# Sixteen DRAM-to-DRAM weight-sum transfers, each tied to one dense unit of the mLSTM stage through an unused column

## The chip, the cores and the metric

The kernel runs on one core of a Trainium2 chip. The metric is device time in microseconds (us), the median of several executions. A core has five engines that run side by side, each through its own instructions in order: TensorE (PE in the profile, its weight loads PEld), VectorE (DVE), ScalarE (ACT), GpSimd (POOL) and SyncE (SP), which here only issues transfers. GpSimd issues transfers too. All transfers share the core's 16 DMA engines; those of SyncE lie in queue q1, those of GpSimd in queue q0.

## The reference

One layer of a streaming encoder for 1024 prompt tokens and 64 sample tokens, 1088 columns in all, with 1024 channels, in float32. Cut to what matters:

```
u    = rmsnorm(x, norm1_g) * (1 + sc1) + sh1          # adaLN: sh, sc, g from silu(c) @ w_ada
proj = u @ w_in                                        # q k v | mq mk | mv mo | i f | ga gb
y_a  = stick_breaking(q, k, v)                         # 8 heads of 64
conv = silu(b_conv + causal width-4 conv of (mq mk))
h    = mlstm(conv_q, conv_k, mv, i, f)                 # 4 heads of 128, running max, chunks
y_b  = sigmoid(mo) * rmsnorm(h) * ml_norm_g
x    = x + g1 * ((sigmoid(ga) * (y_a @ w_a) + sigmoid(gb) * (y_b @ w_b)) @ w_out)
u2   = rmsnorm(x, norm2_g) * (1 + sc2) + sh2
x    = x + g2 * ((silu(u2 @ w_ff_gate) * (u2 @ w_ff_up)) @ w_ff_down)
y    = rmsnorm(x, final_g)
```

The products of the FFN's gate and up matrices (1024 x 2816 each) are computed with seven half-size products in place of eight. Four of the seven need weights that are sums of halves: S1 = up's upper half + up's lower half, S2 = S1 + gate's upper half, S3 = up's upper half + gate's upper half, S4 = S2 + gate's lower half.

## The kernel before, in words

Each matmul is three float32r matmuls (mm3, L76 to L78): high part by high part, high by low, low by high. A *dense unit* (`unit`, L340) computes 128 output channels for all 1088 columns. It loads its weights (`w_unit`, SyncE, tile wr), splits them on GpSimd into wh and wl (L53, L59), and runs 3 chunks of 320, 384 and 384 columns, 24 matmuls each, into one of three PSUM banks of tag d. An `evac` function empties each bank. wr, wh and wl have three buffers each, so the split of a unit waits until TensorE has finished the unit three places earlier, and the load of a unit waits for the split of the unit three places earlier.

The mLSTM stage is the loop over four heads h at L908. The generator `mlstm(h)` does the recurrence of head h (W is its decay table, hn its output, hsq the squares for its norm, ps_yb the transposes of its result) while the dense units q, k, v of attention pair h and mq, mk, mv, mo of head h+1 run as filler (`chain(dense)`; in the last head two adaLN blocks and two gate units take the place of the latter). In TensorE's order the units are thus q0 k0 v0 mq1 mk1 mv1 mo1 q1 k1 v1 mq2 and so on. mq and mk are emptied into xp by ScalarE, and VectorE copies their last three columns before the padding into cvo (L687 from the first chunk, L688 at the end). k, v, mv and mo are emptied by ScalarE into kf, vf, mvf and mog.

For a change of heads, W (one buffer) is loaded from nm_d at L725, as a broadcast of 1152 rows of 512 bytes, as soon as the last read of the W before it is done. VectorE's dc (L727, L728) reads it, then GpSimd adds a mask (L730, nine pieces), ScalarE takes dc (L731) and nine exponentials (L733). Between these, in ScalarE's order, stand the three copies of mo's banks into mog (L713).

The FFN's weight sums for the first ten blocks of 128 channels are made by the DMA engines alone, from DRAM to DRAM: `sum_copy` (L158) copies a half matrix of 512 x 1280 into wsum_d[x], `sum_add` (L168) adds another to it (a transfer with accumulation), each in two transfers of 512 x 640, 1280 KB. Sixteen in all, from GpSimd's queue. So that they don't all start at the beginning, each copy is preceded by a transfer of one element of cvo into the place that the copy overwrites, from the same queue: the copy must wait for it, and it must wait for cvo. The adds have no such element; they wait for the copies. They are placed in the code behind units of heads 1 to 3. The FFN reads wsum_d in `load_pair` (L1250), 80 loads of 256 KB.

The order on each engine isn't that of the code: a scheduler sorts all instructions by priority and its own estimates, and adds the waits.

Of the kernel before, what the change touches and what calls it, by code (L numbers as in the profile page):

```python
# [8 lines left out]
F32 = mybir.dt.float32  # L9
F32R = mybir.dt.float32r  # L10
AF = mybir.ActivationFunctionType
ALU = mybir.AluOpType
AX = mybir.AxisListType

P = 128
NS = 64
NP = 1024
T = NS + NP
D = 1024
# [16 lines left out]
def trunk(ctx, tc, a, o, dbg=None, stop=None):  # L36
    nc = tc.nc
# [5 lines left out]
    dram = ctx.enter_context(tc.tile_pool(name="scr", bufs=1, space=bass.MemoryType.DRAM))  # L43
# [27 lines left out]
    def cols(w, c0, n=P):  # L71

        return w[:, c0 : c0 + n].rearrange("(kb p) n -> p kb n", p=P)
# [20 lines left out]
    w_g, w_u, w_d = a["w_ff_gate"][0], a["w_ff_up"][0], a["w_ff_down"][0]  # L94
# [25 lines left out]
    cvo = const.tile([P, 48], F32, name="cvo")  # L120
# [30 lines left out]

    KH = D // 2
    NFC = NF * P
    wsum_d = {x: dram.tile([KH, NFC], F32, name=f"wsum{x}_d") for x in (1, 2, 3, 4)}
    g1w, g2w, u1w, u2w = w_g[0:KH, 0:NFC], w_g[KH:D, 0:NFC], w_u[0:KH, 0:NFC], w_u[KH:D, 0:NFC]
    sum_parts = {1: (u1w, u2w), 2: (g1w, wsum_d[1]), 3: (u1w, g1w), 4: (g2w, wsum_d[2])}

    def sum_copy(x, b):  # L158

        def go():  # L160
            for c in range(0, NFC, NFC // 2):
                nc.gpsimd.dma_start(wsum_d[x][0:1, c : c + 1], cvo[0:1, b : b + 1])
                nc.gpsimd.dma_start(wsum_d[x][:, c : c + NFC // 2], sum_parts[x][0][:, c : c + NFC // 2])
            return
            yield
        return go()

    def sum_add(x):  # L168
        def go():
            for c in range(0, NFC, NFC // 2):  # L170
                nc.gpsimd.dma_start(wsum_d[x][:, c : c + NFC // 2], sum_parts[x][1][:, c : c + NFC // 2], accum_op=ALU.add)
            return
            yield
        return go()

    def small(shape, name, tag, dtype=F32, bufs=2, pool=None):
        return (pool or cur["sb"]).tile(shape, dtype, tag=tag, name=name, bufs=bufs)
# [135 lines left out]
    pairs = [Pair() for _ in range(4)]  # L313
    heads = [Pair() for _ in range(4)]
# [504 lines left out]
    def qkv_units(p):  # L819
        return [in_unit(f"q{p}", OFF_Q + P * p, (p, 0), evac_qk, alloc_qk),  # L820
                in_unit(f"k{p}", OFF_K + P * p, (p, 1), evac_qk, alloc_qk), k_post(p),
                in_unit(f"v{p}", OFF_V + P * p, (p,), evac_v, alloc_v), v_post(p)]

    def ml_units(h):
        return [in_unit(f"mq{h}", OFF_MQ + P * h, (h, 0), evac_x, alloc_x),
                in_unit(f"mk{h}", OFF_MK + P * h, (h, 1), evac_x, alloc_x),
                in_unit(f"mv{h}", OFF_MV + P * h, (h,), evac_mv, alloc_mv),
                in_unit(f"mo{h}", OFF_MO + P * h, (h,), evac_mo, alloc_mo)]
# [8 lines left out]
    def chain(gens):  # L837
        for g in gens:
            yield from g

    def run(consumer, dense, nsteps, nd):

        n = 0.0
        done = False
        if nd == 0:
            for _ in consumer:
                pass
            done = True
        for _ in dense:
            n += nsteps / max(nd, 1)  # L850
            while n >= 1.0 and not done:
                n -= 1.0
                done = next(consumer, "end") == "end"
        for _ in consumer:
            pass
# [49 lines left out]
    for u in [gates_if()] + ml_units(0)[2:]:  # L905
        for _ in u:
            pass
    for h in range(4):  # L908
        q_, k_, kp, v_, vp = qkv_units(h)
        m_ = ml_units(h + 1) if h < 3 else ada_left[0:2] + gates[0:2]  # L910
        b_ = [[], [sum_copy(1, 1), sum_copy(3, 5), sum_add(1), sum_add(3)], [sum_copy(2, 2), sum_copy(4, 6), sum_add(2)],
              [sum_add(4)]][h]
        dense = []
        for i, g in enumerate([q_, k_, kp, v_, vp] + m_):
            dense += [g] + (b_[i // 2 : i // 2 + 1] if i % 2 == 0 else [])
        run(mlstm(h), chain(dense), 14, 23 if h < 3 else 17)
    ps = bank("t", "ps_cvo", 3)
    nc.tensor.transpose(ps[:48, 0:P], cvo, ident)
# [97 lines left out]
    for m in range(KB):  # L1016
        if m % 2 == 0:
            wh, wl = wide_unit(w_a, 0, 4, m // 2, f"wa{m}")
        for c, (s, e) in enumerate(CHUNKS):
            n = e - s  # L1020
# [10 lines left out]
            for lo, hi in ([(s, HT), (HT, e)] if s < HT < e else [(s, e)]):  # L1031
                h = lo // HT
                src, r = gts[0][:, lo - s : hi - s], slice(lo - HT * h, hi - HT * h)
# [216 lines left out]
    def load_pair(i):  # L1250

        def half(w, r):
            return w[r * KH : (r + 1) * KH, i * P : (i + 1) * P].rearrange("(k p) n -> p k n", p=P)

        res = {}
        if i >= NF:
            raws = []
            for w, nm in ((w_g, "g"), (w_u, "u")):
                raw = wp.tile([P, KB, P], F32, tag="wr", name=f"wr_{nm}{i}")
                nc.sync.dma_start(raw, cols(w, i * P))  # L1260
                raws.append(raw)
            res[1], res[2], res[0], res[4] = raws[0][:, 0:4], raws[0][:, 4:8], raws[1][:, 0:4], raws[1][:, 4:8]
            return res
        src = {1: half(w_g, 0), 6: half(wsum_d[2], 0), 5: half(wsum_d[1], 0), 7: half(wsum_d[3], 0),
               2: half(w_g, 1), 3: half(wsum_d[4], 0), 4: half(w_u, 1)}
        for k in range(4):
            if k < 3:
                raw = wp.tile([P, KB, P], F32, tag="wr", name=f"wr_{k}_{i}")
            else:
                raw = gp.tile([P, 4, P], F32, tag="S1", name=f"wr_{k}_{i}", bufs=1)  # L1270
            for x, p in enumerate(order[2 * k : 2 * k + 2]):
                res[p] = raw[:, 4 * x : 4 * x + 4]
                nc.sync.dma_start(res[p], src[p])
        return res
# [88 lines left out]
    slices = [list(range(NF + 4 * i, NF + 4 * i + 4)) for i in range(3)] + [[0, 1, 2, 3], [4, 5, 6, 7], [8, 9]]  # L1363
    jobs = [(i, (0,)) for i in range(NF)] + [(i, (0, 1)) for i in range(NF, FFB)] + [(i, (1,)) for i in range(NF)]
    raw = load_pair(0)
    ws = {p: weight_op(0, p, raw) for p in order}

# [4 lines left out]
    for k, (i, halves) in enumerate(jobs):  # L1372
        nxt, nxt_i = {}, jobs[k + 1][0] if k + 1 < len(jobs) else None
        if k == FFB:
            todo = chain([early_h(b) for b in slices[0]])

        def hook(p, last):
            if last and raw:
                nxt[p] = weight_op(nxt_i, p, raw)
            if (k < NF and p in (6, 2)) or (k >= FFB and p == 5):  # L1380
                step(todo)

        for h in halves:
            if h == halves[-1]:
                raw = load_pair(nxt_i) if nxt_i is not None else None
            gate_up(i, h, ws, lambda p: hook(p, h == halves[-1]))
        ws = nxt
        if k == NF - 1:
            for _ in todo:
                pass  # L1390
# [74 lines left out]
    sums = {}  # L1465
# [102 lines left out]
```

## Time and profile before

| | us |
|---|---|
| median of 3 runs (1866.32 to 1869.25) | 1866.44 |
| the profiled execution | 1861.14 |
| its span, first to last instruction | 1859.4 |

| in the span | |
|---|---|
| mean granted TensorE clock | 0.979 |
| moved by the DMA engines | 265.51 MB, 143 GB/s |
| share of the 16 DMA engines, queue q1 (SyncE) | 41.1% |
| share of the 16 DMA engines, queue q0 (GpSimd) | 9.0% |

The difference between the execution's time and its span, 1.7 us, lies outside the instructions. The slices of the page (40 of 46.5 us each) show in tenths how busy TensorE and the DMA engines are and the granted clock:

```
PE   6899799999989999988998999999999999999997
PEclk9999899999999999998999999999999999999999
DMA  9427749423485565684566345622222666443102
```

Counted from 0, the mLSTM stage is slices 2 to 10. Of these, TensorE is below 9 tenths in slice 4, and there the clock is lower as well. Idle time of another engine costs nothing while TensorE has work.

### The profile page before, as it was taken

The numbers are of one execution on the slowest core, as the hardware profiler recorded it, in microseconds if no ns is written. First come the engines' busy times: TensorE is split into PE (matmuls) and PEld (weight loads), VectorE is DVE, ScalarE is ACT, GpSimd is POOL, SyncE is SP. The second block draws the span as 40 slices with busy tenths as digits, with TensorE's granted clock in tenths as the row PEclk, the third lists the DMA queues.
The fourth block names the chain that finished last, engine by engine and source line by source line (L and its number), as shares of the span: only waits on it lengthen the run. The fifth ranks groups of instructions, "written<-read, shape, count | busy, mean of one in ns | idle before, by whom it ended". The sixth has DMA issues, their size and how long they took to land. (4 is left out here: it accounts for less than half of the span.)

```text
span 1859.4 us, 31695 instructions
## 1 busy us (share of the span) xinstructions
PE 1763.3 (95%) x12388; PEld 1695.7 (91%) x12388; DVE 995.4 (54%) x1903; ACT 673.5 (36%) x1403; POOL 678.2 (36%) x562
## 2 busy tenths in 40 slices
PE   6899799999989999988998999999999999999997
PEld 4799799899979888877898999999999999999997
DVE  6623314133355758696554389665445776544535
ACT  4433322434234435353412456433233553100006
POOL 3434445335432232368566240032222002354324
PEclk9999899999999999998999999999999999999999
DMA  9427749423485565684566345622222666443102
GB/s 273 104 88 193 193 118 259 131 83 118 128 173 142 136 141 152 157 231 157 156 201 195 93 144 169 197 88 82 86 71 76 194 203 189 168 146 110 55 12 97
DMA packets 313433, 265.51 MB, mean 143 GB/s; under 512 B 13895, under 2 KB 285507, under 8 KB 313283
## 3 DMA queue, kind: packets, MB, share of 16 engines
q1 hardware_dynamic: 300994, 224.67, 41.1%
q0 software_dynamic: 12288, 38.80, 9.0%
q8 instruction: 98, 1.61, 0.4%
q14 instruction: 53, 0.43, 0.1%
HBM read 206.59 MB, written 77.81 MB: 153 GB/s over the span
## 5 line engine op out<-in xcount | busy, mean ns | idle before, releaser
L76 PE MATMUL ps_fd<-hh,wh_fd 128*128 128x384 f32 (+1 forms) x480 | 157.3, 328 | 1.2 <-DVE hst L1336 1.2
L78 PE MATMUL ps_fd<-hh,wl_fd 128*128 128x384 f32 (+1 forms) x480 | 157.4, 328 | 0.0
L77 PE MATMUL ps_fd<-hl,wh_fd 128*128 128x384 f32 (+1 forms) x480 | 157.2, 328 | 0.0
L56 DVE TENSOR_TENSOR w<-wr,w 128x512 fp32r<-128x512 f32 x140 | 96.5, 701 | 40.0 <-ACT w L47 37.1
L1420 DVE SCALAR_TENSOR_TENSOR x1f<-ps_fd,mod,x1f 128x384 f32<-128x384 f32 (+2 forms) x128 | 60.4, 497 | 101.8 <-PE ps_fd L78 101.8
L390 DVE TENSOR_TENSOR_SCAN re<-re 128x128 f32<-128x128 f32 (+3 forms) x64 | 103.6, 1622 | 15.2 <-ACT re L386 14.8
L47 ACT CAST w<-wr 128x512 fp32r<-128x512 f32 x140 | 85.0, 619 | 73.8 <-PE ps_gc L1344 22.8
L53 POOL TENSOR_SCALAR wh_fd<-wr_fd 128x1024 fp32r<-128x1024 f32 x20 | 24.4, 1220 | 227.9 <-PE ps_ga L1344 119.4
L76 PEld LDWEIGHTS ps_fd<-hh,wh_fd 128*128 128x128 f32 x480 | 90.2, 188 | 1.4 <-POOL wl_fd L59 1.4
L78 PEld LDWEIGHTS ps_fd<-hh,wl_fd 128*128 128x128 f32 x480 | 90.2, 188 | 0.0
L77 PEld LDWEIGHTS ps_fd<-hl,wh_fd 128*128 128x128 f32 x480 | 90.2, 188 | 0.0
L47 ACT CAST hh<-hr 128x1088 fp32r<-128x1088 f32 (+1 forms) x26 | 24.0, 961 | 175.2 <-PE ps_fd L77 152.7
L386 ACT ACTIVATE re<-z 128x512 f32<-128x512 f32 (+2 forms) x96 | 47.3, 494 | 83.4 <-DVE z L382 69.8
L1344 PE MATMUL ps_ga<-b1h,w 128*128 128x272 f32 x352 | 74.7, 292 | 2.5 <-ACT g L1329 1.8
L1344 PE MATMUL ps_gb<-b6h,w 128*128 128x272 f32 x352 | 75.0, 292 | 0.4 <-ACT g L1329 0.4
L1344 PE MATMUL ps_gc<-b5h,w 128*128 128x272 f32 x352 | 74.0, 290 | 0.0
L1344 PE MATMUL ps_gd<-b7h,w 128*128 128x272 f32 x352 | 73.9, 290 | 0.0
L1344 PE MATMUL ps_ga<-b2h,w 128*128 128x272 f32 x352 | 73.8, 289 | 0.0
L1344 PE MATMUL ps_gc<-b3h,w 128*128 128x272 f32 x352 | 73.7, 289 | 0.0
L1344 PE MATMUL ps_gd<-b4h,w 128*128 128x272 f32 x352 | 73.6, 289 | 0.0
L76 PE MATMUL ps_ga<-uh,wh_ga 128*128 128x384 f32 (+1 forms) x192 | 64.9, 338 | 1.5 <-DVE re L388 1.1
L56 DVE TENSOR_TENSOR al<-ps_a,ah 128x512 fp32r<-128x512 f32 (+1 forms) x80 | 49.4, 629 | 30.3 <-ACT ah L47 30.1
(552 smaller groups left out, 6072.4 us busy)
## 6 DMA issues: line engine op xcount, KB each, us to landing
wada<-in_w_ada SPq DMA_DIRECT2D x48, 512.0 KB
wr<-wsum_d SPq DMA_DIRECT2D x80, 256.0 KB
h_d<-hst SPq DMA_DIRECT2D x44, 272.0 KB
wr<-in_w_ff_gate SPq DMA_DIRECT2D x40, 256.0 KB
wr_fd<-in_w_ff_down SPq DMA_DIRECT2D x20, 512.0 KB
hr<-h_d SPq DMA_DIRECT2D x18, 544.0 KB
wsum_d<-in_w_ff_up POOLq DMA_DIRECT2D x6, 1280.0 KB, 12.3
wsum_d<-in_w_ff_gate POOLq DMA_DIRECT2D x6, 1280.0 KB, 11.8
```

The lines of the kernel that those rows point to most:

```text
L47: nc.scalar.copy(out, in_)
L53: nc.gpsimd.tensor_scalar(out, in_, 1.0, 0.0, ALU.mult, ALU.add)
L56: nc.vector.tensor_sub(out, in_, h.bitcast(F32))
L76: nc.tensor.matmul(ps, wh, xh, start=first, stop=False)
L77: nc.tensor.matmul(ps, wh, xl, start=False, stop=False)
L78: nc.tensor.matmul(ps, wl, xh, start=False, stop=last)
L386: nc.scalar.activation(rest[:, c0 : c0 + w], ps, AF.Sigmoid, scale=-scale)
L390: nc.vector.tensor_tensor_scan(r, r, r, 1.0, ALU.mult, ALU.bypass)
L1344: nc.tensor.matmul(ps, w[:, a, j, :], b[j // 2][:, j % 2, :], start=p in (1, 6, 5, 7) and j == 0 and k == 0, stop=j == 3 and k == 2, skip_ ...
L1420: nc.vector.scalar_tensor_tensor(x1[m][:, lo:hi], ps[:, lo - s : hi - s], mod[:, 40 + m, g : g + 1], x1[m][:, lo:hi], ALU.mult, ALU.add)
```

## The change

The two halves of each wsum_d tensor become 512 rows of 641 elements each, and so does the source of each transfer: 640 that are used and one column that nobody reads. Every one of the sixteen transfers, the adds too, is preceded by a one-element transfer into that column of its first row. This transfer is issued from SyncE, and its source is an element that the dense unit just finished has written: the last column of kf, vf, mvf or mog, or a column of cvo. The sixteen pairs stand one by one behind the units k, v, mq, mk, mv, mo of head 0, the same of head 1, and k, v, mq, mk of head 2. `load_pair` reads the new layout.

```diff
@@ -151,27 +151,27 @@
 
     KH = D // 2
     NFC = NF * P
-    wsum_d = {x: dram.tile([KH, NFC], F32, name=f"wsum{x}_d") for x in (1, 2, 3, 4)}
-    g1w, g2w, u1w, u2w = w_g[0:KH, 0:NFC], w_g[KH:D, 0:NFC], w_u[0:KH, 0:NFC], w_u[KH:D, 0:NFC]
-    sum_parts = {1: (u1w, u2w), 2: (g1w, wsum_d[1]), 3: (u1w, g1w), 4: (g2w, wsum_d[2])}
-
-    def sum_copy(x, b):
-
-        def go():
-            for c in range(0, NFC, NFC // 2):
-                nc.gpsimd.dma_start(wsum_d[x][0:1, c : c + 1], cvo[0:1, b : b + 1])
-                nc.gpsimd.dma_start(wsum_d[x][:, c : c + NFC // 2], sum_parts[x][0][:, c : c + NFC // 2])
-            return
-            yield
-        return go()
-
-    def sum_add(x):
-        def go():
-            for c in range(0, NFC, NFC // 2):
-                nc.gpsimd.dma_start(wsum_d[x][:, c : c + NFC // 2], sum_parts[x][1][:, c : c + NFC // 2], accum_op=ALU.add)
-            return
-            yield
-        return go()
+    HC = NFC // 2
+
+
+    wsum_d = {x: dram.tile([KH, 2, HC + 1], F32, name=f"wsum{x}_d") for x in (1, 2, 3, 4)}
+
+    def wpart(w, half, c):
+        return w[half * KH : (half + 1) * KH, c * HC : (c + 1) * HC + 1]
+
+    sum_parts = {1: ((w_u, 0), (w_u, 1)), 2: ((w_g, 0), 1), 3: ((w_u, 0), (w_g, 0)), 4: ((w_g, 1), 2)}
+
+    def sum_step(x, k, c, when):
+
+        nc.sync.dma_start(wsum_d[x][0:1, c, HC : HC + 1], when())
+        src = sum_parts[x][k]
+        src = wsum_d[src][:, c, :] if isinstance(src, int) else wpart(*src, c)
+        if k:
+            nc.gpsimd.dma_start(wsum_d[x][:, c, :], src, accum_op=ALU.add)
+        else:
+            nc.gpsimd.dma_start(wsum_d[x][:, c, :], src)
+        return
+        yield
 
     def small(shape, name, tag, dtype=F32, bufs=2, pool=None):
         return (pool or cur["sb"]).tile(shape, dtype, tag=tag, name=name, bufs=bufs)
@@ -905,14 +905,23 @@
     for u in [gates_if()] + ml_units(0)[2:]:
         for _ in u:
             pass
+
+    sums = [(x, k, c) for x, k in ((1, 0), (3, 0), (1, 1), (2, 0), (2, 1), (3, 1), (4, 0), (4, 1)) for c in range(2)]
     for h in range(4):
         q_, k_, kp, v_, vp = qkv_units(h)
         m_ = ml_units(h + 1) if h < 3 else ada_left[0:2] + gates[0:2]
-        b_ = [[], [sum_copy(1, 1), sum_copy(3, 5), sum_add(1), sum_add(3)], [sum_copy(2, 2), sum_copy(4, 6), sum_add(2)],
-              [sum_add(4)]][h]
+        def last(t):
+            return t[0:1, T - 1 : T]
+
+        said = [None, lambda h=h: last(pairs[h].kf), None, lambda h=h: last(pairs[h].vf), None]
+        if h < 3:
+            said += [lambda h=h: cvo[0:1, h + 1 : h + 2], lambda h=h: cvo[0:1, h + 5 : h + 6],
+                     lambda h=h: last(heads[h + 1].vf), lambda h=h: last(heads[h + 1].og)]
         dense = []
         for i, g in enumerate([q_, k_, kp, v_, vp] + m_):
-            dense += [g] + (b_[i // 2 : i // 2 + 1] if i % 2 == 0 else [])
+            dense.append(g)
+            if i < len(said) and said[i] and sums:
+                dense.append(sum_step(*sums.pop(0), said[i]))
         run(mlstm(h), chain(dense), 14, 23 if h < 3 else 17)
     ps = bank("t", "ps_cvo", 3)
     nc.tensor.transpose(ps[:48, 0:P], cvo, ident)
@@ -1252,6 +1261,10 @@
         def half(w, r):
             return w[r * KH : (r + 1) * KH, i * P : (i + 1) * P].rearrange("(k p) n -> p k n", p=P)
 
+        def summed(x):
+            c, o_ = divmod(i * P, HC)
+            return wsum_d[x][:, c, o_ : o_ + P].rearrange("(k p) n -> p k n", p=P)
+
         res = {}
         if i >= NF:
             raws = []
@@ -1261,8 +1274,7 @@
                 raws.append(raw)
             res[1], res[2], res[0], res[4] = raws[0][:, 0:4], raws[0][:, 4:8], raws[1][:, 0:4], raws[1][:, 4:8]
             return res
-        src = {1: half(w_g, 0), 6: half(wsum_d[2], 0), 5: half(wsum_d[1], 0), 7: half(wsum_d[3], 0),
-               2: half(w_g, 1), 3: half(wsum_d[4], 0), 4: half(w_u, 1)}
+        src = {1: half(w_g, 0), 6: summed(2), 5: summed(1), 7: summed(3), 2: half(w_g, 1), 3: summed(4), 4: half(w_u, 1)}
         for k in range(4):
             if k < 3:
                 raw = wp.tile([P, KB, P], F32, tag="wr", name=f"wr_{k}_{i}")
```

How this moves instructions is shown at three places. First SyncE, at the change from head 0 to head 1 (W is head 1's table; wr_mq and wr_mk are the weights of head 2's units; wsum_d<-cvo and the like are the one-element transfers). Before:

```order
L64 DMA wr_v_2429<-in_w_in 128x8x128
L64 DMA wr_mq_2581<-in_w_in 128x8x128
L725 DMA W_2278<-nm_d 128x9x128
L64 DMA wr_mk_2703<-in_w_in 128x8x128
L773 DMA out_C_prompt<-co_8_1952 128x128
L64 DMA wr_mv_2827<-in_w_in 128x8x128
L802 DMA yb_d<-yb_2059 128x1088
```

and now:

```order
L64 DMA wr_v_2435<-in_w_in 128x8x128
L166 DMA wsum_d<-cvo 1x1
L64 DMA wr_mq_2587<-in_w_in 128x8x128
L725 DMA W_2286<-nm_d 128x9x128
L166 DMA wsum_d<-mvf_1889 1x1
L64 DMA wr_mk_2711<-in_w_in 128x8x128
L773 DMA out_C_prompt<-co_8_1960 128x128
L166 DMA wsum_d<-mog_2016 1x1
L64 DMA wr_mv_2835<-in_w_in 128x8x128
```

Three one-element transfers now stand among the loads, and wr_mk, wr_mv and the stores behind them are issued only after the element is there. yb's store has moved further back.

Second GpSimd, over the same stretch (wh and wl are the split weights of mo, q and k; hsq belongs to head 0's norm, W to head 1). Before:

```order
L171 DMA wsum_d<-in_w_ff_up 512x640
L162 DMA wsum_d<-cvo 1x1 x2
L171 DMA wsum_d<-in_w_ff_up 512x640
L163 DMA wsum_d<-in_w_ff_up 512x640 x2
L53 TENSOR_SCALAR wh_q_2104<-wr_q_2102 128x1024
L59 TENSOR_TENSOR wl_q_2105<-wr_q_2102,wh_q_2104 128x1024
L171 DMA wsum_d<-in_w_ff_gate 512x640 x2
L53 TENSOR_SCALAR wh_k_2223<-wr_k_2221 128x1024
L59 TENSOR_TENSOR wl_k_2224<-wr_k_2221,wh_k_2223 128x1024
L786 TENSOR_TENSOR hsq_1988<-hn_1361 128x1152
L730 TENSOR_TENSOR W_2278<-W_2278,mmask 128x128 x9
```

and now:

```order
L172 DMA wsum_d<-in_w_ff_up 512x641
L53 TENSOR_SCALAR wh_q_2116<-wr_q_2114 128x1024
L59 TENSOR_TENSOR wl_q_2117<-wr_q_2114,wh_q_2116 128x1024
L53 TENSOR_SCALAR wh_k_2231<-wr_k_2229 128x1024
L59 TENSOR_TENSOR wl_k_2232<-wr_k_2229,wh_k_2231 128x1024
L730 TENSOR_TENSOR W_2286<-W_2286,mmask 128x128 x9
L170 DMA wsum_d<-in_w_ff_up 512x641
L786 TENSOR_TENSOR hsq_1996<-hn_1361 128x1152
```

The queue of eight transfers ahead of and among the splits of q and k is down to one, the fourth of the sixteen (the first row). The fifth, an add, stands behind the W pieces. hsq, which stood ahead of the W pieces, stands behind both.

Third TensorE, where the transposes ps_yb of head 0 stand among the matmuls of unit q of pair 1 (uh and ul are the halves of the input, numbered by block). Before:

```order
L76 MATMUL ps_q_0_2108<-uh_133,wh_q_2104 128x320
L77 MATMUL ps_q_0_2108<-ul_134,wh_q_2104 128x320
L799 MATMUL ps_yb_0_2060<-ident,hn_1361 128x64
L799 MATMUL ps_yb_0_2060<-ident,hn_1361 128x128 x2
L799 MATMUL ps_yb_1_2065<-ident,hn_1361 128x128 x3
L799 MATMUL ps_yb_2_2070<-ident,hn_1361 128x128 x3
L78 MATMUL ps_q_0_2108<-uh_133,wl_q_2105 128x320
```

and now:

```order
L76 MATMUL ps_q_2_2198<-uh_123,wh_q_2116 128x384
L77 MATMUL ps_q_2_2198<-ul_124,wh_q_2116 128x384
L799 MATMUL ps_yb_0_2070<-ident,hn_1361 128x64
L799 MATMUL ps_yb_0_2070<-ident,hn_1361 128x128 x2
L799 MATMUL ps_yb_1_2075<-ident,hn_1361 128x128 x3
L799 MATMUL ps_yb_2_2080<-ident,hn_1361 128x128 x3
L78 MATMUL ps_q_2_2198<-uh_123,wl_q_2117 128x384
```

The nine transposes have moved from the first chunk of q (ps_q_0) to the third (ps_q_2), 33 matmuls later. In ScalarE's order the nine exponentials of W now stand together ahead of the second and third mog copy, as they did before at the change from head 2 to head 3. The change from head 1 to head 2 is altered in the same way.

## The prediction

> **What bounds the kernel now.** The first view is the page's busy table, then the list of who waited for whom, cut to the mLSTM stage (80 to 520 us), with total wait, number of waits and longest one.
>
> ```profile
> PE 1763.3 (95%) x12388; PEld 1695.7 (91%) x12388; DVE 995.4 (54%) x1903; ACT 673.5 (36%) x1403; POOL 678.2 (36%) x562
> PE ps_q L76 <- POOL W L730: 11.8, 2, 8.6
> PE ps_yb L799 <- DVE hn L790: 7.8, 3, 4.1
> ```
>
> TensorE is the bound, so an edit elsewhere pays only where TensorE stands still. In this stage it does so on two lines that repeat by head: the first matmuls of a q unit, and the nine transposes ps_yb. The timeline of TensorE shows where (start, duration, then in brackets the idle time before and its releaser). First the matmul pitch at full clock, then the two gaps, each from the last ps_mo matmul to the first ps_q one that runs undisturbed:
>
> ```profile
> 196.14 0.31 PE L76 MATMUL ps_mo<-uh,wh_mo 128*128 128x320 f32 x1
> 198.63 0.31 PE L78 MATMUL ps_mo<-uh,wl_mo 128*128 128x320 f32 x1
> ...
> 207.04 0.34 PE L78 MATMUL ps_mo<-uh,wl_mo 128*128 128x384 f32 x1
> 215.97 0.60 PE L76 MATMUL ps_q<-uh,wh_q 128*128 128x320 f32 x1 [8.59 <-POOL W L730]
> 224.07 2.27 PE L799 MATMUL ps_yb<-ident,hn 64*128 64x64 f32 x9 [3.28 <-DVE hn L790]
> 227.74 0.34 PE L76 MATMUL ps_q<-uh,wh_q 128*128 128x384 f32 x1
> 227.92 0.34 PE L77 MATMUL ps_q<-ul,wh_q 128*128 128x384 f32 x1
> ...
> 319.90 0.34 PE L78 MATMUL ps_mo<-uh,wl_mo 128*128 128x384 f32 x1
> 323.49 0.61 PE L76 MATMUL ps_q<-uh,wh_q 128*128 128x320 f32 x1 [3.25 <-POOL W L730]
> 331.59 2.26 PE L799 MATMUL ps_yb<-ident,hn 64*128 64x64 f32 x9 [4.05 <-DVE hn L790]
> 336.74 0.34 PE L77 MATMUL ps_q<-ul,wh_q 128*128 128x384 f32 x1
> ```
>
> Idle time is 8.59 + 3.28 + 3.25 + 4.05 = 19.2 us. The matmuls behind it are also slower (0.60 instead of 0.31); the windows view (sum, then TensorE, weight load, VectorE, ScalarE, GpSimd, granted clock, DMA share, GB/s) gives the clock there:
>
> ```profile
> 216.00:220.80 4.80, 4.79 (x17) 4.44 (x17) 0.15 (x1) 4.74 (x7) 4.72 (x6) 0.52 0.25 65
> ```
>
> So each gap costs its idle time and a stretch at about half clock. What ends the gaps, by SyncE, VectorE and ScalarE, in the order of time, for both heads:
>
> ```profile
> 191.88 0.37 SPq L725 DMA_DIRECT2D W<-nm_d  x1
> 213.59 0.18 DVE L727 TENSOR_TENSOR dc<-W,mcb 128x8 f32<-128x8 f32 x1 [15.60 <-DMA W<-nm_d]
> 215.39 0.44 ACT L713 ACTIVATE mog<-ps_mo 128x320 f32<-128x320 f32 x1
> ...
> 303.80 0.53 SPq L725 DMA_DIRECT2D W<-nm_d  x1
> 321.11 0.17 DVE L727 TENSOR_TENSOR dc<-W,mcb 128x8 f32<-128x8 f32 x1 [10.29 <-DMA W<-nm_d]
> ```
>
> TensorE's wait is put down to a GpSimd row, but the chain starts at a transfer: W, the next head's decay table, was issued at 191.88 and landed at 213.59, 21.7 us later. VectorE stood at dc; ScalarE, which reads dc next, stood too, and behind that in its queue the emptying of ps_mo's first bank (ended 215.83), which TensorE needs for q. In head 2, W took 17.3 us. The third such change of heads is the control:
>
> ```profile
> 412.18 0.37 SPq L725 DMA_DIRECT2D W<-nm_d  x1
> 419.27 0.89 DVE L727 TENSOR_TENSOR dc<-W,mcb 128x8 f32<-128x8 f32 x1 [1.55 <-DMA W<-nm_d]
> 427.78 0.49 ACT L713 ACTIVATE mog<-ps_mo 128x384 f32<-128x384 f32 x1
> 428.49 0.31 PE L76 MATMUL ps_q<-uh,wh_q 128*128 128x320 f32 x1
> 435.60 1.30 PE L799 MATMUL ps_yb<-ident,hn 64*128 64x64 f32 x9
> ```
>
> W lands in 7.1 us and TensorE never waits. What differs is what shares the DMA engines. In head 1's change GpSimd issues two copies at 184 and two adds behind them, the last at 198; the last of all sixteen goes out at 310.8, a hundred microseconds before the control. The rows are GpSimd's issues, the tile view of wsum_d (least, median and longest issue in ns, first and last start), and the queue table of 155 to 235 us, which gives the price of eight transfers (packets, MB, share of 16 engines):
>
> ```profile
> 184.19 1.28 POOL L163 DMA_DIRECT2D wsum_d<-in_w_ff_up  x2 [6.90 <-DMA wsum_d<-cvo]
> 198.44 1.03 POOL L171 DMA_DIRECT2D wsum_d<-in_w_ff_gate  x1 [2.66 <-DMA wsum_d<-in_w_ff_up]
> L171 POOL DMA_DIRECT2D wsum_d<-wsum_d x4: 1035/1062/1070, 283.9 to 310.8; - x4
> q0 software_dynamic: 3328, 10.49, 53.6%
> ```
>
> 53.6% of 80 us is 42.9 us of all 16 engines, 5.4 us for each transfer, and they stand in a row around W.
>
> **The change part by part.** *Spacing.* Each of the 16 transfers now waits for its own one-element transfer on SyncE, and that for one dense unit. In head 0 these are k0, v0, mq1, mk1, mv1, mo1. The fourth is the last ahead of W: the cvo column that it reads is written in the first row here, and the second has the landing of the eight small transfers of before:
>
> ```profile
> 173.56 0.16 DVE L687 COPY cvo<-xp 128x3 f32<-128x3 f32 x1
> DMA to landing us min/median/max: 2.4/6.3/10.1
> 195.45 0.48 ACT L707 COPY mvf<-ps_mv 128x384 f32<-128x384 f32 x1
> 203.06 0.37 SPq L64 DMA_DIRECT2D wr_mk<-in_w_in  x1
> ```
>
> So the fourth starts between 176 and 184, by the two ends of that row, and at 5.4 us of engine time is done before 191.9 in both cases; I take 177, near the short end, since SyncE's queue isn't behind the sums themselves. The fifth stands behind the nine W adds on GpSimd, so it can't start before W has landed. The same holds one and two heads later. W should then take what the control shows, 7.1 us, and the chain after it too. From W's landing to the end of the second mog copy the control took 428.27 − 419.27 = 9.0 us, and the new ScalarE order there is that of the control. In head 1 that gives 191.9 + 7.1 + 9.0 = 208.0, while q's second chunk would start at 207.2 + 24 × 0.147 = 210.7. Margin 2.7 us.
>
> *The sum.* Gap 1: from 207.21 (one pitch of 0.17 after the last ps_mo) to 227.74 are 20.5 us, for 24 matmuls at 0.147 (2.49 us over 17 in the rows) and nine transposes (1.3 in the control), 4.8 us. Excess 15.7. Gap 2: 320.07 to 336.74 are 16.7 us for 3.5 + 1.3 + 4 × 0.17 = 5.5. Excess 11.2. Together **26.9 us**, 19.2 of it idle and 7.7 slow clock. I take all of it. TensorE carries the end from there on, and no later stage waits on a point fixed in time, so nothing should give it back. If some other transfer still delays W past the margin, the gain shrinks by that delay in each head.
>
> *What is added on SyncE.* Behind a waiting small transfer stand weight loads (wr_mk behind the one that reads mvf, wr_mv behind mog). mvf is written by 195.93, and wr_mk went out at 203.06, because its buffer is free only when GpSimd has split the unit before. The small transfer asks for the same unit that frees the buffer, so the loads lose between 0 and about 1 us each; the next use of wr_mk lies two units later. I take 0.
>
> *On GpSimd.* Eight small issues go. The sixteen large ones stay, one at a time; hsq now stands behind the nine W adds and one of them (1.05 us). The control shows the slack of the chain behind hsq:
>
> ```profile
> 428.64 1.01 DVE L788 TENSOR_SCALAR mx<-mx 128x9 f32<-128x9 f32 x1
> 430.50 0.21 ACT L83 ACTIVATE rs_h<-mx 128x9 f32<-128x9 f32 x1
> 432.79 1.36 DVE L790 TENSOR_TENSOR hn<-hn,rd 128x1152 f32<-128x1152 f32 x1
> ```
>
> mx was there at 429.65, 0.8 us before ScalarE, busy with mog, took it; hn was there at 434.15, 1.4 us before the transposes at 435.60; and they now stand two matmuls into q's third chunk, about 0.9 us later still. So 3.1 us of slack stand against 1.05 us plus what is left of the small transfer's landing. I take 0, the bound is 2 us in each of two heads. Below nothing I see only the third ps_yb wait, under 1 us.
>
> *The unused column.* Rows in wsum_d are 641 elements long, so most rows start at odd places, for the transfers and for the 80 loads in the FFN. The trace of before has no such access. The nearest rows are the FFN's:
>
> ```profile
> wr<-wsum_d SPq DMA_DIRECT2D x80, 256.0 KB
> 1450.00:1500.00 50.00, 50.00 (x400) 50.00 (x399) 36.07 (x69) 26.39 (x50) 0.00 (x0) 1.00 0.69 212
> 1500.00:1550.00 50.00, 50.00 (x400) 50.00 (x399) 34.99 (x65) 24.89 (x48) 0.00 (x0) 1.00 0.68 203
> ACT w L47 <- DMA wr<-wsum_d: 2.2, 4, 0.9
> ```
>
> TensorE is full at a DMA share of 0.69, and those loads were waited for 2.2 us in all. About half of the share, 0.34, is theirs (four of seven loads, seven of 262 KB in each 10 us, are 183 of 208 GB/s). They may take up to 1.9 times as long before the share reaches 1.0. I take 0 here.
>
> The Trainium skill speaks against the column: "DMA: Bandwidth & Descriptors", section "How a descriptor splits into AXI transactions", says that a run which doesn't start on a 256-byte boundary fetches from the boundary below it. By that page a 512-byte run costs about 20 beats instead of 16 on average, an estimate; the share would rise to about 0.77, and the sum would stay as it is. No row here shows it.
>
> **Rivals.**
> 1. *W still meets a transfer.* If a transfer lasts so long that W needs 13 us, in all three heads: mog ends at 213.9 against 210.7, 3.2 us of idle, and by gap 2 (3.25 idle, then ten matmuls at 0.27 instead of 0.147) another 1.2 to 1.5 of clock; some 4.6 us a head, 14 in all. For it: adds move more than copies, and the third head now has transfers too. Against: 14 us or so between the last two units ahead of W, 5.4 us a transfer. Time: 1853.
> 2. *The FFN becomes bound by DMA, slower than before.* Place: 1100 to 1200 and 1450 to 1550 us. It decides from a factor of 1.9 on. At 2.5 the share would be 0.69 + 1.5 × 0.34 = 1.20, 200 us grow by 40, less 26.9: 1879. For it: no row bounds the misplaced reads. Against: the 0.31 of free share.
> 3. *The change doesn't do it:* W is late for another reason, such as its own 1152 short rows, or the small transfers fire all at once. Time: 1866. Against: the control, same load, same rows, 7.1 us.
>
> Rival 1's clock term has another price in the Trainium skill, "TensorE: Matmul & The Clock Gate", Part 1: the clock falls after an idle window of about 3.4 us, so 3.2 us would cost the idle alone and the time would be about 1849. The trace differs: 3.25 us of idle were enough at 323.49.
>
> **How the numbers follow.** The profiled execution took 1861.1 us (span 1859.4). Less 26.9 it is 1834.2. The runs' median is 1866.4, 5.3 more than that execution; I carry the difference over: **1839.5**. Forecast 0.78, rival 1 0.10, rival 2 0.06, rival 3 0.06. The low end is 1834: if the 5.3 us of the timed runs lie in these gaps, they go as well. The high end is rival 1, 1853, which also covers the 4 us of hsq. Faster by over 0.2% (3.7 us, what a measurement here can tell from no change): 0.88; within: 0.06; slower: 0.06.
>
> **What would show it.** W landing 7 to 9 us after its issue in all three heads, no bracket of idle time at ps_q, ps_yb's wait below 1 us each, granted clock 1.0 in the windows of the two gaps, wsum transfers one at a time, 6 us or more apart. Wrong would be: W above 12 us; idle on TensorE before a q, k or v unit released by GpSimd weight splits (the loads held up on SyncE); DMA share near 1.0 with TensorE waiting for w between 1100 and 1550.

## The result and the profile after

| | before | after |
|---|---|---|
| median, 4 runs each (range) | 1866.38 us (1861.42 to 1869.25) | 1839.17 us (1834.28 to 1842.75) |
| the profiled execution (its span) | 1861.14 us (1859.4) | 1842.75 us (1841.1) |
| first to fourth load of W | 296.73 us | 269.76 us |

The ratio is 0.9855 (95% interval 0.9824 to 0.9887), 27.2 us less in the medians; 1839.5 was predicted. First the page's busy table of after, then all its waits of TensorE from 80 to 500 us (total, number, longest):

```profile
PE 1759.8 (96%) x12388; PEld 1693.1 (92%) x12388; DVE 1006.8 (55%) x1903; ACT 671.0 (36%) x1401; POOL 677.5 (37%) x554
...
PE z L520 <- DMA kh<-qk_d: 3.0, 1, 3.0
PE ps_ift L581 <- ACT ifr L577: 2.8, 2, 2.2
PE ps_c L902 <- DVE C_s L903: 2.2, 1, 2.2
PE z L521 <- DMA kl<-qk_d: 0.6, 1, 0.6
PE ps_yb L799 <- DVE hn L790: 0.5, 1, 0.5
```

The ps_q line is gone and ps_yb is down to one wait of half a microsecond, at the end of the last head; the other rows lie ahead of the heads or in the attention behind them. What went shows in the windows view from the first to the fourth load of W (sum, then busy time of TensorE, weight load, VectorE, ScalarE and GpSimd, then granted clock, DMA share, GB/s). Before:

```profile
115.45:412.18 296.73, 277.56 (x1727) 272.67 (x1727) 87.80 (x185) 100.44 (x224) 125.62 (x119) 0.96 0.60 163
```

and after:

```profile
118.62:388.38 269.76, 269.76 (x1727) 265.65 (x1727) 98.65 (x185) 97.83 (x222) 124.33 (x111) 1.00 0.67 179
```

Before, TensorE stood still for 19.2 us of the stage, and the same 1727 matmuls kept it busy 7.8 us longer, at a mean clock of 0.96. After, it is busy all the time at clock 1.00. The timeline of SyncE and VectorE at the three changes of heads:

```profile
194.10 0.36 SPq L725 DMA_DIRECT2D W<-nm_d  x1
200.46 1.61 DVE L727 TENSOR_TENSOR dc<-W,mcb 128x8 f32<-128x8 f32 x1 [0.82 <-DMA W<-nm_d]
...
291.18 0.36 SPq L725 DMA_DIRECT2D W<-nm_d  x1
297.24 1.92 DVE L727 TENSOR_TENSOR dc<-W,mcb 128x8 f32<-128x8 f32 x1 [0.52 <-DMA W<-nm_d]
...
388.38 0.36 SPq L725 DMA_DIRECT2D W<-nm_d  x1
395.32 1.03 DVE L727 TENSOR_TENSOR dc<-W,mcb 128x8 f32<-128x8 f32 x1 [1.40 <-DMA W<-nm_d]
```

W is there after 6.4, 6.1 and 6.9 us, where it took 21.7, 17.3 and 7.1. The rest of the chain, on ScalarE, TensorE and VectorE in the first of these:

```profile
209.70 0.49 ACT L713 ACTIVATE mog<-ps_mo 128x384 f32<-128x384 f32 x1
213.90 0.34 PE L76 MATMUL ps_q<-uh,wh_q 128*128 128x384 f32 x1
214.71 1.36 DVE L790 TENSOR_TENSOR hn<-hn,rd 128x1152 f32<-128x1152 f32 x1
218.53 1.30 PE L799 MATMUL ps_yb<-ident,hn 64*128 64x64 f32 x9
```

The second mog copy ends at 210.19, 16.1 us after W's issue, and q's second chunk starts at 213.90: 3.7 us of margin. hn is ready at 216.07, 2.5 us ahead of the transposes. The windows view over the places of the two old gaps, its columns as above:

```profile
200.00:230.00 30.00, 30.00 (x190) 29.61 (x189) 13.74 (x23) 16.56 (x31) 23.03 (x19) 1.00 0.81 187
310.00:340.00 30.00, 30.00 (x189) 28.60 (x189) 8.54 (x19) 10.44 (x23) 14.75 (x9) 1.00 0.75 192
```

TensorE is full at clock 1.0 although the DMA engines are busy for three quarters of the time and more.

In the two profiled executions the span fell by 18.3 us only. First to fourth W gives 26.97; the start up to the first W took 3.2 longer (115.45 before, 118.62 after; a second profile of before, before2 below, has 118.55, so this is scatter), and from the fourth W to the end 5.5 (1447.2, then 1452.7). The profiled execution of after was the slowest of its four. What the 5.5 are is a question to the experiments.

### The profile page after: what moved, and what is told of

Read it like the earlier page. It is cut to its first block, busy times and chain, and to the rows that moved or that the text cites. A ratio compares the mean times of both kernels' runs of the same rounds, so it can differ in the third digit from the quotient of the medians.

```text
span 1841.1 us, 31721 instructions
## 1 busy us (share of the span) xinstructions
PE 1759.8 (96%) x12388; PEld 1693.1 (92%) x12388; DVE 1006.8 (55%) x1903; ACT 671.0 (36%) x1401; POOL 677.5 (37%) x554
## 5 line engine op out<-in xcount | busy, mean ns | idle before, releaser
L56 DVE TENSOR_TENSOR al<-ps_a,ah 128x512 fp32r<-128x512 f32 (+1 forms) x80 | 49.4, 630 | 34.2 <-ACT ah L47 33.8
```

The costliest lines, as they stand in the source:

```text
L56: nc.vector.tensor_sub(out, in_, h.bitcast(F32))
```

## The experiments

Theory: W was late because the sums' transfers stood around it in a row; spacing them brings it back, and nothing else in the change costs or gains. Rivals: the layout, the queue (SyncE), or the ties as such do it, or other places pay. All ratios are to the kernel before, with their 95% intervals; "stage" is the first to the fourth load of W.

**layout**: the kernel before with rows of 641 elements, its ties and places as they were.

```diff
-    wsum_d = {x: dram.tile([KH, NFC], F32, name=f"wsum{x}_d") for x in (1, 2, 3, 4)}
+    wsum_d = {x: dram.tile([KH, 2, HC + 1], F32, name=f"wsum{x}_d") for x in (1, 2, 3, 4)}
...
-                nc.gpsimd.dma_start(wsum_d[x][0:1, c : c + 1], cvo[0:1, b : b + 1])
+                nc.gpsimd.dma_start(wsum_d[x][0:1, c, 0:1], cvo[0:1, b : b + 1])
```

> The kernel before with the new layout alone: rows of 641 elements with the unread column, transfers of 512 x 641 and the FFN's loads from them, but the old one-element transfers on GpSimd's queue at the old places. If only the spacing pays (theory): 1866 +- 4, both gaps at the change of heads remain, W lands about 22 and 17 us after its issue. If the layout has a price of its own (rival): 5 us or more slower, by longer landings and a third gap.

Measured: 1869.83 us, ratio 1.0029 (1.0006 to 1.0052). VectorE's timeline:

```profile
211.35 0.17 DVE L735 TENSOR_TENSOR dc<-W,mcb 128x8 f32<-128x8 f32 x1 [15.04 <-DMA W<-nm_d]
...
325.83 0.17 DVE L735 TENSOR_TENSOR dc<-W,mcb 128x8 f32<-128x8 f32 x1 [17.22 <-DMA W<-nm_d]
```

W, issued at 189.81 and 302.07, took 21.5 and 23.8 us; the stage took 301.5. The layout alone gains nothing; the kernel is 0.3% slower with it.

**aligned**: the changed kernel with rows 704 elements apart in wsum_d, of which 641 are written, so that in wsum_d each row starts at a multiple of 256 bytes.

```diff
-    wsum_d = {x: dram.tile([KH, 2, HC + 1], F32, name=f"wsum{x}_d") for x in (1, 2, 3, 4)}
+    wsum_d = {x: dram.tile([KH, 2, HC + 64], F32, name=f"wsum{x}_d") for x in (1, 2, 3, 4)}
```

> The changed kernel, but each half row of wsum_d lies on a pitch of 704 elements (2816 bytes) in place of 641, so that the rows the FFN loads start where a 256-byte block starts; the transfers still carry 641 elements. If the odd starts cost nothing (my theory): within 3 us of the changed kernel's 1839, ratio to before 0.985 +- 0.003, mLSTM stage and FFN as there. If the odd starts slow the transfers or the FFN's loads (rival): 5 us or more faster than the changed kernel, with shorter landings of the sums.

Measured: 1840.05 us, 0.9867 (0.9829 to 0.9905), stage 269.77. Odd starts cost nothing that shows in the time. In the FFN of after the windows of the prediction read

```profile
1450.00:1500.00 50.00, 50.00 (x401) 50.00 (x400) 35.68 (x68) 24.99 (x47) 0.00 (x0) 1.00 0.73 212
1500.00:1550.00 50.00, 50.00 (x401) 50.00 (x400) 34.22 (x65) 23.23 (x45) 3.21 (x3) 1.00 0.67 197
```

The mean share is 0.70, where before had 0.685; but after is some 19 us further on in the FFN at these times. Over 430 us from about the FFN's first matmul on (before from 1100, after from 1081, aligned from 1082) the share is 0.44 in all three. By the Trainium skill ("DMA: Bandwidth & Descriptors", "How a descriptor splits into AXI transactions") the estimate for the two windows was 0.77. At most a small part of that shows, and the time doesn't contain it.

**nosums**: the kernel before without any of the transfers. The FFN reads plain halves in the place of the four sums, so its output lacks them.

```diff
-        b_ = [[], [sum_copy(1, 1), sum_copy(3, 5), sum_add(1), sum_add(3)], [sum_copy(2, 2), sum_copy(4, 6), sum_add(2)],
-              [sum_add(4)]][h]
+        b_ = []
```

> The kernel before without the sixteen transfers and their eight one-element ones; the FFN loads plain halves of the weights in their place, the same 80 loads, so that the output of the FFN is left wrong by that part. Theory (the transfers cost only through W): W lands in 7 us in all heads, no gap, the stage from the first W issue to the fourth takes 270 us as in the changed kernel, and the time is within 3 us of it, 1839. Rival (the spaced transfers still cost something by contention): 1830 or less.

Measured: 1837.66 us, 0.9855 (0.9814 to 0.9896); W 7.3, 6.3 and 6.3 us; stage 269.78, with TensorE busy for all of it at clock 1.00. This is the floor of the stage for anything done to these transfers, and the changed kernel stands on it: its stage is the same to 0.02 us.

**bunch**: the changed kernel, its layout, its SyncE queue and its element for each transfer, but six, six and four steps together behind mk of heads 0, 1 and 2.

```diff
-            if i < len(said) and said[i] and sums:
-                dense.append(sum_step(*sums.pop(0), said[i]))
+            if i == 6 and h < 3:
+                for _ in range(6 if h < 2 else 4):
+                    dense.append(sum_step(*sums.pop(0), said[6]))
```

> The changed kernel with the six steps of heads 0 and 1 and the four of head 2 all placed behind unit mk and tied to mk's cvo element, so that they start together some 17 us ahead of W. Layout, one-element transfers on SyncE and their number are those of the changed kernel. Theory (W's landing is what matters): six transfers of 5.4 us of engine time each reach past W's issue, W lands 13 to 20 us after it in heads 1 to 3, TensorE stands still at ps_q or ps_yb in at least two of the three changes of heads, 8 to 30 us in all: 1848 to 1870. Rival (the transfers on SyncE or the layout made the gain, not the spacing): as the changed kernel, 1839 +- 3.

Measured: 1875.18 us, 1.0055 (1.0036 to 1.0073), above the range expected. TensorE's waits in the stage, W on VectorE, and the windows while it waits:

```profile
PE ps_q L76 <- ACT mog L713: 25.3, 2, 14.3
PE ps_yb L799 <- DVE hn L790: 5.6, 3, 3.2
PE ps_q L76 <- ACT co L772: 5.3, 1, 5.3
...
215.72 0.17 DVE L727 TENSOR_TENSOR dc<-W,mcb 128x8 f32<-128x8 f32 x1 [19.72 <-DMA W<-nm_d]
...
190.00:215.00 25.00, 17.14 (x106) 16.78 (x105) 1.09 (x6) 1.68 (x4) 5.59 (x4) 0.90 1.01 224
302.00:331.00 29.00, 17.37 (x108) 17.02 (x106) 1.31 (x6) 2.96 (x5) 5.40 (x4) 0.86 1.07 206
```

W took 25.0, 28.3 and 19.4 us: now all three changes of heads have their gap, the one that was the control too. The share of the DMA engines is full over each stretch. Same layout, same queue, one tie for each transfer: what differs is that all ties of a head hang on one unit, and that takes back all of the gain. This tells spacing from the rest of the change. (The scheduler orders the other instructions anew in each kernel; but VectorE stood still until W landed, as the row above shows, so it is the landing that became late.)

**early**: the same bunches behind unit k, some 50 us ahead of W.

```diff
+            if i == 1 and h < 3:
+                for _ in range(6 if h < 2 else 4):
+                    dense.append(sum_step(*sums.pop(0), said[1]))
```

> The changed kernel with the steps of a head (six, six, four) all placed behind unit k and tied to kf's last element, so that they start together some 50 us ahead of W in place of 17. As bunched as the run before (6 x 5.4 = 32 us of engine time in a row), but over before W is issued. Theory (what counts is that no sum is in flight when W is): W lands in 6 to 8 us, no idle time on TensorE at ps_q or ps_yb, 1839 +- 4. Rival (the even spreading counts, since weight loads of the units meet the sums): idle time before a q, mv or mo unit, 1845 or more.

Measured: 1845.59 us, 0.9905 (0.9873 to 0.9938). W took 6.7, 6.6 and 7.2 us, as the theory has it, but the stage took 277.46, 7.7 us above the floor: something else stands now. The time is the rival's, but the place is not: TensorE's long wait is at none of the units that it named. ScalarE's and TensorE's timelines:

```profile
267.47 0.26 ACT L367 COPY vn<-ps_nat_v 64x128 f32<-64x128 f32 x1 [11.19 <-DMA out_k_prompt<-kn]
268.05 0.78 PE L744 MATMUL ps_S<-cv,cv 128*128 128x128 f32 x2 [4.89 <-ACT vn L368]
...
268.00:273.00 5.00, 4.95 (x23) 4.95 (x24) 2.29 (x4) 3.52 (x7) 4.92 (x8) 0.66 0.87 139
```

kn and vn take turns in a buffer. The store of kn to the output, issued at 243.72 when four of the head's six transfers had just gone out, was slowed as W had been; ScalarE, with vn next in its order, waited 11.2 us for it; TensorE needs the bank that ScalarE empties and stood 4.9 us. The clock fell to 0.66 behind that (last row, windows). In the changed kernel ScalarE doesn't wait for this store at all. Moving the bunch moves the victim.

**again**, **again2** and **before2**: the changed kernel twice more, the kernel before once more.

> The changed kernel unaltered, a second profile of it. From the first W issue to the fourth 269.8 us as in the first. From there to the end its first profile took 1452.7 us against 1447.2 before; if that is chance (theory), it lies anywhere between 1445 and 1457 here; if the change costs something later on (rival), 1452 or more again. Time 1836 to 1843.

> The changed kernel a third time. Theory (the later loss is the change's): fourth load of W to the end 1452 us or more, as in the two profiles so far (1452.7 and 1454.4). Rival (scatter): under 1450 us. First to fourth load of W 269.8 us by both.

> The kernel before once more, for the scatter of one profile to the next. Theory (the later loss is the change's): fourth load of W to the end 1446 to 1449 us as in the first profile (1447.2). Rival (scatter): 1450 us or more here, or under 1450 in the repeat of the changed kernel.

Measured: again 1838.40 us, 0.9877 (0.9839 to 0.9916), stage 269.77; again2 1838.25 us (one run), stage 269.77; before2 1866.91 us (one run), W 23.1 and 19.6 us, stage 300.96. From the fourth W to the end again took 1454.4, which both of its expectations allow; again2 took 1450.4, between its two; before2 took 1445.7, just below its theory. So the three decide nothing about the later loss; the table below takes them up.

**tagpool**: the one-element transfers from GpSimd's queue.

```diff
-        nc.sync.dma_start(wsum_d[x][0:1, c, HC : HC + 1], when())
+        nc.gpsimd.dma_start(wsum_d[x][0:1, c, HC : HC + 1], when())
```

> The changed kernel with the sixteen one-element transfers issued from GpSimd in place of SyncE, just ahead of their large ones. GpSimd now stands still until each dense unit is done, and the small transfers lie in the queue of the sums. Theory (SyncE is only a cheaper place to wait): splits of weights are held up by 1 to 5 us each and have a unit's time in hand, so 1839 to 1845, W lands in 6 to 8 us. Rival (SyncE's in-order wait costs weight loads something): 1836 or less.

Measured: 1838.68 us, 0.9875 (0.9837 to 0.9912), stage 269.78, W 6.2, 7.7 and 6.7 us. The time is 0.3 us below the theory's range and far from the rival's: the queue makes no difference to the time. Here the landing of the small transfers is on record, which it isn't for those of SyncE. The source views give it in us (least, median, longest), first for the small transfers (L166), then for the copies (L172) and the adds (L170):

```profile
DMA to landing us min/median/max: 1.6/3.0/6.1
...
DMA to landing us min/median/max: 6.2/7.1/8.8
...
DMA to landing us min/median/max: 9.4/11.3/13.6
```

In after the large ones take much the same: 6.2 to 8.0 us for the copies, 9.5 to 14.2 for the adds.

**notag**: the changed kernel without the one-element transfers.

```diff
-        nc.sync.dma_start(wsum_d[x][0:1, c, HC : HC + 1], when())
```

> The changed kernel without the sixteen one-element transfers, so that nothing ties the sums to a unit; the scheduler puts all of them at the head of GpSimd's queue, at the start of the kernel. Theory: no sum is left when W is loaded, so the first W issue to the fourth takes 270 us as in the changed kernel, but the sums (16 x 5.4 = 86 us of all DMA engines) meet the loads of x and of w_ada in the first 100 us, where the DMA share is already 0.9 in the first slice; the first W issue moves from 115 to 118 us to 135 to 180 us, total 1855 to 1900. Rival (the ties are not needed): 1839 +- 4.

Measured: 1910.23 us, 1.0264 (1.0216 to 1.0311), slower than expected. All sums went out ahead of the mLSTM stage, the first at 1.4 us and the last at 138. TensorE's largest waits from 0 to 160 us, and the queue table from 0 to 200:

```profile
PE ps_ada L216 <- DMA wada<-in_w_ada: 25.6, 3, 13.5
PE ps_mx L76 <- POOL uh L53: 25.0, 7, 13.4
PE ps_x L290 <- DVE xt L283: 20.5, 2, 13.2
...
q0 software_dynamic: 6400, 21.01, 44.3%
```

The first W was issued at 190.91 instead of 114 to 119; from there the stage took 269.74, the floor. 44.3% of 200 us are 88.6 us of all 16 engines for 16 transfers, 5.5 each, and 72 to 77 us of it lengthened the start. So the sums cost nothing in a stage that has room and most of their length in one that waits for its loads. Ties are needed; that each hangs on a unit of its own is what makes them even (bunch has a tie for each transfer too).

**eight** and **drop4** ask where the 5.5 us behind the stage come from. eight puts all sixteen into heads 0 and 1, in pairs behind units k and v and singly behind mq, mk, mv and mo. drop4 is the changed kernel without the four steps of head 2, with the plain second half of the gate in the place of that sum.

```diff
-            if i < len(said) and said[i] and sums:
-                dense.append(sum_step(*sums.pop(0), said[i]))
+            if h < 2 and i < len(said) and said[i]:
+                for _ in range(2 if i in (1, 3) else 1):
+                    dense.append(sum_step(*sums.pop(0), said[i]))
```

> The sixteen steps tied in the changed kernel's way, but all in the first two heads (two steps behind mk and two behind mv, one behind each of the other four units), none in head 2. It looks at the 4 to 6 us that the changed kernels lose between the fourth load of W and the end of the span (1452.7, 1454.4, 1456.1 and 1451.1 us against 1447.2 before). Theory (the transfers in flight in head 2 push the stages behind out of step): fourth load of W to the end within 1446 to 1449 us, first to fourth load 269.7 to 272 us, median 1834 to 1837 us, ratio to before 0.983 to 0.986. Rival (it is scatter between runs, or the new layout): 1450 to 1456 us, median 1838 to 1841 us.

(The expectation names the units of the pairs as mk and mv; it is units k and v, as in the edit.)

> The changed kernel without its last four steps, those tied in head 2; the FFN takes the plain second half of the gate weights in the place of that sum, so the FFN's output lacks this part. All else is the changed kernel. Theory (the transfers in head 2 cost the later stages): fourth load of W to the end 1446 to 1449 us, median 1834 to 1837 us. Rival (scatter, or the layout and the ties as such): 1450 to 1456 us, median 1838 to 1841 us.

Measured: eight 1846.41 us, 0.9905 (0.9878 to 0.9932), outside both ranges; drop4 1838.54 us, 0.9862 (0.9826 to 0.9898), the rival's. eight's stage took 277.3 us:

```profile
262.56 0.26 ACT L367 COPY vn<-ps_nat_v 64x128 f32<-64x128 f32 x1 [8.02 <-DMA out_k_prompt<-kn]
...
PE ps_S L744 <- ACT vn L368: 4.2, 1, 4.2
```

This is early's stall, and here one pair is enough for it: the two adds behind unit k of head 1, issued at 242.73 and 243.40, the second landing at 261.92. kn's store, issued at 247.57, was waited for until 262.56. So two transfers behind one unit can already be too dense for this stage; one behind each costs it nothing.

From the fourth load of W to the end of the span, in us, worked out for each profile:

| no tie for each transfer | | a tie for each transfer | |
|---|---|---|---|
| before, before2 | 1447.2, 1445.7 | after, again, again2 | 1452.7, 1454.4, 1450.4 |
| layout | 1449.2 | tagpool, aligned | 1451.1, 1456.1 |
| nosums | 1447.5 | early, eight | 1450.0, 1452.2 |
| notag | 1447.3 | drop4 | 1453.5 |

(bunch is left out: its third gap lies there.) The columns don't overlap; the means are 5.2 us apart (1452.6 against 1447.4). So in the profiled executions something is lost there. It isn't the layout (layout and notag have it), and it isn't transfers in head 2 (eight and drop4 have none there). From 20 us behind the fourth W on, the orders of TensorE, ScalarE and GpSimd are in after those of before, and VectorE's differs in two places of 1541. Nor is it the FFN: from its first matmul (ps_ga<-b1h) to the end all fourteen profiles take 759.4 to 761.4 us, odd rows or not, while from the fourth W to that matmul those of the left column take 684.8 to 688.4 and those of the right 689.0 to 695.3. It isn't one wait either: in these rows of TensorE, 280 to 360 us behind the fourth W, before and after differ by one or two microseconds at a time.

```profile
PE po L541 <- DVE al L56: 1.8, 2, 1.1
PE ps_a L534 <- DVE be L391: 1.2, 2, 0.7
PE ps_ys L503 <- DVE ys L501: 0.4, 1, 0.4
```

```profile
PE ps_a L534 <- DVE be L391: 2.7, 4, 1.2
PE ps_ys L503 <- DVE ys L501: 2.3, 1, 2.3
PE po L541 <- DVE al L56: 1.5, 1, 1.5
```

Above is before, below after. In the medians the loss doesn't show (nosums 1837.66 us, drop4 1838.54, again 1838.40). The profiled execution was the slowest of its kernel's in after, again, aligned, drop4 and eight, and the fastest in nosums, which would make the loss scatter; but it was the fastest in tagpool and early too, and these stand in the right column with 1451.1 and 1450.0. Whether it is the change's or scatter stays open.

A second buffer for W, so that it could be loaded a head ahead, was not tried.

## Why the prediction was right, step by step

- **W is the cause and the transfers around it are the reason.** Right, and shown: nosums without them and after with them spaced have W in 6.1 to 7.3 us and the same stage; bunch with them together has 19 to 28 us in all three heads.
- **The sum, 26.9 us.** The stage lost 26.97: 19.2 of idle time and 7.8 of slow clock, against 19.2 and 7.7 in the sum, and the clock is 1.0 in both windows. The size holds for the execution that was read; before2's stage, 300.96, would have given 31.2.
- **The chain behind W.** 7.1 + 9.0 = 16.1 us from W's issue to the second mog copy was predicted, and 16.1 measured; the margin of 2.7 us was 3.7.
- **The fourth transfer ahead of W.** Start between 176 and 184, 177 taken; it went at 180.88, 13 us ahead of W where the prediction had 15. The cvo element is written from 177.75, 4.2 us later than before, and 3.2 of these are the longer start of this execution. For the small transfer's landing the prediction took the short end of 2.4 to 10.1 us because SyncE's queue isn't behind the sums; that was right here: 2.95 us after the small transfer's issue the large one goes. GpSimd stood for it, as the timeline of VectorE, SyncE and GpSimd and the idle list of the tile view show:

```profile
177.75 0.15 DVE L687 COPY cvo<-xp 128x3 f32<-128x3 f32 x1
177.93 0.24 SPq L166 DMA_DIRECT2D wsum_d<-cvo  x1
180.88 0.66 POOL L172 DMA_DIRECT2D wsum_d<-in_w_ff_up  x1 [4.21 <-DMA wsum_d<-cvo]
207.02 1.01 POOL L170 DMA_DIRECT2D wsum_d<-in_w_ff_up  x1
207.72 2.45 POOL L786 TENSOR_TENSOR hsq<-hn 128x1152 f32<-128x1152 f32 x1
...
  DMA wsum_d<-cvo: 33.8, 6
```

  These 33.8 us of GpSimd, six waits for cvo and the small transfer behind it, cost the stage nothing: it took what it takes without any transfers (269.76 against 269.78).
- **SyncE's loads held up: 0.** Right. No row of TensorE's waits names a weight split, and tagpool, which takes the small transfers off SyncE, gives the same stage.
- **hsq behind an add: 0 within 2 us a head.** Right: at the first change hn was 2.5 us early, against 3.1 less 1.05 in the prediction, and at no change of heads does TensorE wait for it.
- **Odd rows: 0.** Right, by aligned against after and by the FFN's length, which is the same in all profiles to 2 us.
- **The rivals.** W above 13 us (1853), the FFN bound by DMA (1879), nothing gained (1866): none came.
- **Nothing gives it back later.** True of the medians; in the profiled executions 5.2 us are lost behind the stage, cause open. The step from a profiled execution to the median is the weak one: the prediction carried 5.3 us over, while after's profiled execution lay 3.6 above its median. The medians' difference (27.2) met the sum, the profiles' (18.4) didn't. That the forecast met the median to 0.3 us is in part luck: before2, at 1866.91 us close to the median, had 4.2 us more in the gaps than the execution that was read, and these went too, while the stretch behind the stage was longer in all profiles of the changed kernel.

## What to carry to other kernels

Bulk transfers that nobody waits for can still set the time, through a small load that is waited for: look at how long that load takes from issue to landing with and without the bulk beside it, and take the run without as the floor. Then spread the bulk with one tie for each transfer, each to a different place of the program; a bunch that is moved elsewhere finds another victim (W in bunch, the store of kn in early and eight, the loads of the start in notag). A tie may land late and cost nothing, as long as its engine has slack behind it.

## What was not expected of the hardware

- An element of 4 bytes took 1.6 to 6.1 us to land from GpSimd's queue in tagpool (median 3.0), with at most one sum under way, and 2.4 to 10.1 us in before, where the sums stood in a row.
- Adds fill the DMA engines at fewer bytes than copies: over bunch's waits the share was full at 206 and 224 GB/s. In notag's start, by its rate list in slices of 5 us, it was 363 to 398 from 5 to 30 us, while copies ran beside other loads, and about 210 from 50 to 75, while adds did:

```profile
DMA  3999999999999999999999999387944300030038
GB/s 112 397 364 398 363 390 339 283 316 236 210 210 212 210 210 270 289 291 222 235 214 191 293 291 291 74 141 148 178 88 128 109 0 3 0 105 0 3 77 216
```

  The queue of the sums alone, from 10 to 30 us and from 50 to 75 (packets, MB, share of 16 engines):

```profile
q0 software_dynamic: 890, 4.32, 59.6%
...
q0 software_dynamic: 1749, 4.36, 92.0%
```

  Worked out for a share of 100%, that is 362 GB/s for copies and 190 GB/s for adds, each transfer's 1.31 MB counted once.
- A store to the output that ScalarE doesn't wait for in the changed kernel kept it 11.2 us in early and 8.0 in eight, through a buffer that the next tile shares, and TensorE behind it 4.9 and 4.2 us.
